# One matmul of each pair in the up projection reads and writes its 512 columns in runs of 64, 16 or 4

## The chip, the cores and the metric

The kernel runs on one core of one Trainium2 chip. The metric is device time in microseconds (us) of one execution, and the number compared is the median over several runs. The profile is of one execution of the same program, taken by the hardware profiler.

## What is computed

One layer of a transformer trunk on 256 tokens of width 2048, in float32: two groups of attention heads on one common projection, then an MLP, then a norm. The part that the change touches is the first product of the MLP, `m @ w_up`:

```python
m = rms_norm(h, mlp_norm)                 # (256, 2048)
h = h + jnp.square(relu(m @ w_up)) @ w_down   # w_up: 2048 x 8192, w_down: 8192 x 2048
return rms_norm(h, final_norm)
```

The MLP's two weight matrices hold 2 x 67 MB and make up most of the 184 MB that the kernel reads.

## The kernel before, in words

**Two halves for each number.** Every product is made in TensorE's fp32r type. So that little precision is lost, each float32 number is split into a hi part (the number rounded to fp32r) and a lo part (the rest, again fp32r). Activations lie transposed, with 128 rows of the model dimension on the partitions, and side by side in the free dimension stand the 256 hi values of the 256 tokens and then their 256 lo values: 512 columns for each block of 128 rows (`split_scaled`, L131, and `split`, L136). Weights come from HBM in parts of 128 x 1024 (`load_part`, L96): a DMA brings the float32 part, ScalarE writes its hi (L101), VectorE its lo (L102).

**One chunk is a pair of matmuls** (`mm_chunk`, L108). With 128 x 128 weights, the first matmul of the pair (L111) takes the hi weights and streams all 512 columns, hi and lo halves of the activations, into the 512 float32 columns of a PSUM bank. The second (L113) takes the lo weights and streams only the 256 hi columns, and it adds to the second half of the bank. A tile (`mm_tile`, L116) is 16 such pairs for the 16 blocks of 2048 rows, all accumulated in one bank. After it `evac_sum` (L126) copies the second half out with ScalarE and VectorE adds the first half.

**The MLP** (L687 to L733) goes through the hidden dimension in four quarters of 2048 (`qd` = 0 to 3). For each quarter, 16 up tiles of 16 pairs are made (tile names `up0_0` to `up3_15`), relu and square are applied, the result is split again into the tiles `us` (tags B and C), and then 16 down tiles (`dn`) of 16 pairs are made and added to the residual `h`. In all, the up projection has 4 x 16 x 16 = 1024 pairs, 256 in a quarter.

**What sets the order.** The instructions are written in program order, and the tile framework adds the semaphores. Weights pass through pools of four buffers each (raw, hi, lo), and four PSUM banks hold dense tiles, so loading and splitting run ahead of TensorE until a buffer is missing.

**The end of the kernel.** The last two down tiles are made apart (L735 to L793). Line 748 makes their lo products: the moving operand is 256 columns lying side by side. Line 741 (`hi_pass`) makes their hi products for one block of 128 tokens: its moving operand is 256 columns too, but in two runs of 128 columns, one from the hi half and one from the lo half, 256 columns apart; its output in PSUM is 256 columns side by side.

In the attention part, line 430 multiplies in plain float32 (not fp32r): two calls of 256 columns for each pair of heads.

Of the kernel before, what the change touches and what calls it, by code (L numbers as in the profile page):

```python
# [16 lines left out]
P = 128  # L17
S = 256
D = 2048
KC = D // P  # L20
# [10 lines left out]
WH = 1024  # L31
# [16 lines left out]
def kernel(  # L48
# [18 lines left out]
    nc = tc.nc  # L67
# [9 lines left out]
    def dense_ps(name):  # L77
        return psd.tile([P, 512], F32, tag="d", name=name)
# [17 lines left out]
    def load_part(src, n, name):  # L96
        raw = wpool.tile([P, WH], F32, tag="raw", name=f"raw_{name}")
        hi = wpool.tile([P, WH], F32R, tag="whi", name=f"hi_{name}")
        lo = wpool.tile([P, WH], F32R, tag="wlo", name=f"lo_{name}")
        nc.sync.dma_start(raw[:, :n], src)  # L100
        nc.scalar.copy(hi[:, :n], raw[:, :n])  # L101
        nc.vector.tensor_tensor(lo[:, :n], raw[:, :n], hi.bitcast(F32)[:, :n], op=ALU.subtract)  # L102
        return hi, lo

    def load_block(src, name):
        return [load_part(src[:, i * WH:(i + 1) * WH], WH, f"{name}_{i}") for i in range(2)]

    def mm_chunk(ps, w, col, act, k, first, last):  # L108
        hi, lo = w[col // WH]
        col = col % WH  # L110
        nc.tensor.matmul(ps[:, 0:2 * S], lhsT=hi[:, col:col + P], rhs=act(k, 0, 2 * S),  # L111
                         start=first, stop=False)
        nc.tensor.matmul(ps[:, S:2 * S], lhsT=lo[:, col:col + P], rhs=act(k, 0, S),  # L113
                         start=False, stop=last)

    def mm_tile(name, w, off, act, ks):  # L116
        ps = dense_ps(name)
        n = len(ks)
        for i, k in enumerate(ks):
            mm_chunk(ps, w, off + i * P, act, k, i == 0, i == n - 1)  # L120
        return ps

    def view(t):
        return lambda k, a, b: t[:, k, a:b]

    def evac_sum(ps, name):  # L126
        t = work.tile([P, S], F32, tag="evt", name=f"t_{name}", bufs=3)
        nc.scalar.copy(t, ps[:, S:2 * S])
        return t
# [6 lines left out]
    def split(dst, src):  # L136
        nc.scalar.copy(dst[:, 0:S], src)
        nc.vector.tensor_tensor(dst[:, S:2 * S], src, dst.bitcast(F32)[:, 0:S], op=ALU.subtract)

    def tmp1(name):  # L140
        return work.tile([P, S], F32, tag="t1", name=name, bufs=5)
# [31 lines left out]
    def square_sum(acc, src, first, name, eng=nc.gpsimd):  # L173
        if first:
            nc.scalar.activation(acc, src, AF.Square)
        else:
            sq = work.tile([P, S], F32, tag="sq", name=f"sq_{name}", bufs=2)
            nc.scalar.activation(sq, src, AF.Square)
            eng.tensor_tensor(acc, acc, sq, op=ALU.add)
# [25 lines left out]
    def bcast_ps(v, name):  # L205
        ps = misc_ps(f"bc_{name}")
        for b in range(2):
            dg = work.tile([P, P], F32, tag="diag", name=f"dg_{name}_{b}", bufs=2)
            nc.vector.tensor_scalar(dg, ident, v[:, b:b + 1], None, op0=ALU.mult)
            nc.tensor.matmul(ps[:, b * P:(b + 1) * P], lhsT=ones, rhs=dg, start=True, stop=True)  # L210
        return ps

    def mean_eps(acc_row, n, name):
        ps = token_sums(acc_row, name)
        v = small(f"ms_{name}")
        nc.vector.tensor_scalar(v, ps[:, 0:2], 1.0 / n, EPS, op0=ALU.mult, op1=ALU.add)
        return v
# [38 lines left out]
    for gi, (c0, n) in enumerate(GROUPS):  # L256
        if gi < 2:
            w = [load_part(w_in0[:, c0 * 512:(c0 + n) * 512], n * 512, f"in0_{c0}")]
        nc.sync.dma_start(h[:, c0:c0 + n, :], xT[:, c0:c0 + n, :])
        if gi == 0:  # L260
            nc.sync.dma_start(g_sb, params)
        if gi >= 2:
            w = [load_part(w_in0[:, c0 * 512:(c0 + n) * 512], n * 512, f"in0_{c0}")]
        for c in range(c0, c0 + n):
            split_scaled(xs[:, c, :], h[:, c, :], g_sb[:, G_ATTN + c:G_ATTN + c + 1])
        for c in range(c0, c0 + n):
            for j in range(4):
                mm_chunk(ps0[j], w, (c - c0) * 512 + j * P, xsv, c, c == 0, c == KC - 1)
        if 1 <= gi <= 5:
            buckets(gi - 1)  # L270
        if gi in (2, 4, 6, 8):
            x_squares(gi // 2 - 1)
# [232 lines left out]
    for i in range(15):  # L505
# [8 lines left out]
        w = load_block(w_in[i], f"in{i}")  # L514
        ps = mm_tile(f"in{i}", w, 0, xsv, list(range(KC)))
# [32 lines left out]
    for b in range(2):  # L548
        w = load_block(w_kn[b], f"kn{b}")
        for j in range(4):  # L550
            ps = mm_tile(f"kn{b}_{j}", w, j * 512, kvv, list(range(LC)))
# [3 lines left out]
    for b in range(2):  # L555
        w = load_block(w_v[b], f"v{b}")
        for tb in range(2):
            ps = dense_ps(f"v{b}_{tb}")
            for k in range(LC):
                hi, lo = w[k // 2]  # L560
# [82 lines left out]
    for n, (b, j) in enumerate((b, j) for b in range(3) for j in range(4)):  # L643
        if j == 0:
            w = load_block(w_q_b[b], f"qb{b}")
        ps = mm_tile(f"qb{b}_{j}", w, j * 512, cqv, list(range(LC)))
# [6 lines left out]
        while todo and n >= todo[0][0]:  # L653
            _, jj, rp = todo.pop(0)
# [4 lines left out]
    def residual(ps, mt):  # L659
        nc.vector.tensor_tensor(h[:, mt, :], ps[:, 0:S], h[:, mt, :], op=ALU.add)  # L660
        nc.vector.tensor_tensor(h[:, mt, :], ps[:, S:2 * S], h[:, mt, :], op=ALU.add)
# [3 lines left out]
    for half in range(2):  # L665
        for b in range(8):
            w = load_block(w_out[half, b], f"wo{half}_{b}")
            for j in range(2):
                mt = 2 * b + j
                ps = mm_tile(f"wo{half}_{mt}", w, j * 1024, view(ys[1 - half]), list(range(8)))  # L670
# [11 lines left out]
    msv = view(ms_box[0])  # L682
# [4 lines left out]
    for qd in range(NQ):  # L687
        us = [big.tile([P, 8, 2 * S], F32R, tag=tg, name=f"us{tg}{qd}") for tg in ("B", "C")]

        def usv(k, a, b, us=us):  # L690
            return us[k // 8][:, k % 8, a:b]

        for j in range(QC):
            w = load_block(w_up[qd * QC + j], f"up{qd}_{j}")
            ps = mm_tile(f"up{qd}_{j}", w, 0, msv, list(range(KC)))
            t = evac_sum(ps, f"up{qd}_{j}")
            nc.vector.tensor_tensor(t, ps[:, 0:S], t, op=ALU.add)
            u = tmp1(f"u{qd}_{j}")
            nc.vector.scalar_tensor_tensor(u, t, 0.0, t, op0=ALU.max, op1=ALU.mult)
            split(us[j // 8][:, j % 8, :], u)  # L700
            if qd == 0 and j == 2:
                v = mean_eps(accm, D, "m")
                nc.vector.tensor_copy(dsm, v)
                dps = bcast_ps(v, "m")
                dm = tmp1("dm")
                nc.vector.tensor_copy(dm, dps[:, 0:S])
            if qd == 0 and 4 <= j < 8:
                k = 4 * (j - 4)
                nc.gpsimd.tensor_tensor(h[:, k:k + 4, :], h[:, k:k + 4, :],
                                        dm.unsqueeze(1).broadcast_to([P, 4, S]), op=ALU.mult)  # L710
        tail = KC - 2 if qd == NQ - 1 else KC
        head = [(load_block(w_down[qd, mt], f"dn{qd}_{mt}"), dense_ps(f"dn{qd}_{mt}"))
                for mt in range(2)]
        for mt, ks in ((0, range(15)), (1, range(4)), (0, range(15, QC)), (1, range(4, QC))):
            w, ps = head[mt]
            for k in ks:
                mm_chunk(ps, w, k * P, usv, k, k == 0, k == QC - 1)
        for mt in range(tail):
            if mt < 2:
                ps = head[mt][1]  # L720
            else:
                w = load_block(w_down[qd, mt], f"dn{qd}_{mt}")
                ps = mm_tile(f"dn{qd}_{mt}", w, 0, usv, list(range(QC)))
            residual(ps, mt)
            if qd == NQ - 1:
                if fin is None:
                    fin = big.tile([P, 2, 2, KC, P], F32, tag="A", name="fin")
                square_sum(acch, h[:, mt, :], mt == 0, f"f{mt}", nc.vector)
                if mt == 1:
                    nc.scalar.activation(warm, acch[:, 0:1], AF.Sqrt)  # L730
                nc.scalar.activation(fin[:, 0, :, mt, :],
                                     h[:, mt, :].rearrange("p (b c) -> p b c", b=2), AF.Copy,
                                     scale=g_sb[:, G_FIN + mt:G_FIN + mt + 1])  # L733
# [11 lines left out]
    for mt, w, ps in last:  # L745
        o = misc_ps(f"dn_lo{mt}")[:, 0:S]
        for k in range(QC):
            nc.tensor.matmul(o, lhsT=w[k // 8][1][:, (k % 8) * P:(k % 8 + 1) * P],
                             rhs=us[k // 8][:, k % 8, 0:S], start=(k == 0), stop=(k == QC - 1))
# [145 lines left out]
```

## Time and profile before

| | |
|---|---|
| median of 3 runs | 1037.45 us |
| all runs | 1034.93, 1037.45, 1048.86 us |
| span of the profiled execution, first to last instruction | 1034.7 us |
| TensorE matmul busy | 1007.2 us, 97% of the span |
| VectorE busy | 713.2 us, 69% |
| ScalarE busy | 540.3 us, 52% |
| GpSimd busy | 109.6 us, 11% |
| read from HBM | 183.7 MB |

The profiled execution's own time is known by its span, 1034.7 us. The lowest run is 0.2 us above it and the median 2.8 us. In the trace, a matmul's duration covers its way through the array and overlaps the next one: a 512-column matmul is shown with 391 ns, but the next begins after 230 ns. What a stream of matmuls takes is therefore read from start to start, in the timeline or in the chain of waits.

### The profile page before, as it was taken

How to read it: one execution, taken by the hardware profiler on the slowest of the kernel's cores; microseconds unless marked ns; L12 is line 12 of the kernel's file. 1: busy time of each engine (PE TensorE's matmuls, PEld its weight loads, DVE VectorE, ACT ScalarE, POOL GpSimd, SP SyncE). 2: the span in 40 equal slices, each digit the busy share in tenths (PEclk: the TensorE clock that was granted, in tenths of full speed). 3: DMA queues.
4: the chain of work that ended last, by engine and by line, in shares of the span. 5: the costliest groups of instructions: out<-in, count | busy, mean ns of one | idle time of the engine just before them, and what ended most of it. 6: DMA issues, size and time to landing. Idle time of an engine off the chain costs nothing.

```text
span 1034.7 us, 15469 instructions
## 1 busy us (share of the span) xinstructions
PE 1007.2 (97%) x5830; PEld 881.8 (85%) x5830; DVE 713.2 (69%) x1123; ACT 540.3 (52%) x893; POOL 109.6 (11%) x117
## 2 busy tenths in 40 slices
PE   6889899999999999999999999999999999999997
PEld 5768788889888888888888888888888888888887
DVE  7985888698897866556666656566666556666664
ACT  7464898875664444333444433344443334445553
POOL 4222321452132200000000000000000000000000
PEclk9999999999999999999999999999999999999999
DMA  7579434564455655655656555556655656666652
GB/s 261 171 227 245 133 113 128 168 195 142 153 189 167 204 185 186 198 185 193 191 186 192 194 183 191 193 186 190 194 186 190 195 185 189 196 185 190 194 167 82
DMA packets 53163, 188.94 MB, mean 183 GB/s; under 512 B 6065, under 2 KB 6449, under 8 KB 52833
## 3 DMA queue, kind: packets, MB, share of 16 engines
q1 hardware_dynamic: 51696, 182.54, 55.2%
q0 software_dynamic: 1392, 5.41, 2.2%
q8 instruction: 46, 0.75, 0.3%
q14 instruction: 29, 0.23, 0.1%
HBM read 183.70 MB, written 4.23 MB: 182 GB/s over the span
## 4 chain that ended last, share of the span: by engine, by line
PE 88%; DMA 4%; DVE 3%; ACT 2%; issue 1%; SPq 0%; POOL 0%; POOLq 0%; ACTq 0%; DVEq 0%
PE up L111 23%; PE dn L111 22%; PE up L113 12%; PE dn L113 11%; PE wo L111 6%; PE wo L113 3%; PE in L111 2%; DMA raw_in<-in_w_in_dram 2%; DMA bias<-bias_scratch 2%; PE in L113 1%; DVE lo_in L102 1%; PE dn L741 1%; PE yp L430 1%; PE kn L111 1%; DVE buck L235 1%
## 5 line engine op out<-in xcount | busy, mean ns | idle before, releaser
L111 PE MATMUL up<-ms,hi_up 128*128 128x512 f32 x1024 | 355.8, 392 | 0.0
L113 PE MATMUL up<-ms,lo_up 128*128 128x256 f32 x1024 | 286.8, 280 | 0.0
L102 DVE TENSOR_TENSOR lo_up<-raw_up,hi_up 128x1024 fp32r<-128x1024 f32 x128 | 161.2, 1260 | 115.0 <-ACT hi_up L101 114.5
L101 ACT CAST hi_dn<-raw_dn 128x1024 fp32r<-128x1024 f32 x128 | 135.0, 1054 | 200.8 <-PE dn L111 160.7
L101 ACT CAST hi_up<-raw_up 128x1024 fp32r<-128x1024 f32 x128 | 134.6, 1052 | 178.0 <-issue 133.8
L111 PEld LDWEIGHTS up<-ms,hi_up 128*128 128x128 f32 x1024 | 191.5, 187 | 42.2
L102 DVE TENSOR_TENSOR lo_dn<-raw_dn,hi_dn 128x1024 fp32r<-128x1024 f32 x128 | 156.9, 1226 | 96.3 <-ACT hi_dn L101 91.0
L113 PEld LDWEIGHTS up<-ms,lo_up 128*128 128x128 f32 x1024 | 193.5, 189 | 0.0
L111 PE MATMUL dn<-usB,hi_dn 128*128 128x512 f32 x496 | 174.9, 391 | 0.0
L111 PE MATMUL dn<-usC,hi_dn 128*128 128x512 f32 x496 | 174.9, 391 | 0.0
L113 PE MATMUL dn<-usB,lo_dn 128*128 128x256 f32 x496 | 138.9, 280 | 0.0
L113 PE MATMUL dn<-usC,lo_dn 128*128 128x256 f32 x496 | 138.9, 280 | 0.0
L111 PE MATMUL in<-xs,hi_in 128*128 128x512 f32 x304 | 111.4, 406 | 9.4 <-DVE xs L133 8.6
L111 PEld LDWEIGHTS dn<-usB,hi_dn 128*128 128x128 f32 x496 | 92.8, 187 | 20.3
L111 PEld LDWEIGHTS dn<-usC,hi_dn 128*128 128x128 f32 x496 | 92.8, 187 | 20.3
L113 PEld LDWEIGHTS dn<-usB,lo_dn 128*128 128x128 f32 x496 | 93.7, 189 | 0.0
L113 PEld LDWEIGHTS dn<-usC,lo_dn 128*128 128x128 f32 x496 | 93.7, 189 | 0.0
L111 PE MATMUL wo<-ys,hi_wo 128*128 128x512 f32 x256 | 91.1, 398 | 0.0
L113 PE MATMUL in<-xs,lo_in 128*128 128x256 f32 x304 | 86.8, 287 | 3.1 <-DVE lo_in L102 3.1
L111 PEld LDWEIGHTS in<-xs,hi_in 128*128 128x128 f32 x304 | 58.5, 193 | 23.3 <-DVE xs L133 8.0
L113 PE MATMUL wo<-ys,lo_wo 128*128 128x256 f32 x256 | 72.2, 283 | 0.0
L113 PEld LDWEIGHTS in<-xs,lo_in 128*128 128x128 f32 x304 | 58.8, 194 | 5.4 <-DVE lo_in L102 4.6
(295 smaller groups left out, 1217.9 us busy)
## 6 DMA issues: line engine op xcount, KB each, us to landing
raw_up<-in_w_up_dram SPq DMA_DIRECT2D x128, 512.0 KB, 4.4
raw_dn<-in_w_down_dram SPq DMA_DIRECT2D x128, 512.0 KB, 4.4
raw_in<-in_w_in_dram SPq DMA_DIRECT2D x37, 512.0 KB, 5.5
raw_wo<-in_w_out_dram SPq DMA_DIRECT2D x32, 512.0 KB, 3.8
raw_qb<-in_w_q_b_dram SPq DMA_DIRECT2D x6, 512.0 KB, 4.3
bias_scratch<-biasT POOLq DMA_DIRECT2D x4, 512.0 KB, 5.1
bias<-bias_scratch POOLq DMA_DIRECT2D x4, 512.0 KB, 9.8
raw_kn<-in_w_kn_dram SPq DMA_DIRECT2D x4, 512.0 KB, 4.1
```

What stands on the lines that cost most here:

```text
L101: nc.scalar.copy(hi[:, :n], raw[:, :n])
L102: nc.vector.tensor_tensor(lo[:, :n], raw[:, :n], hi.bitcast(F32)[:, :n], op=ALU.subtract)
L111: nc.tensor.matmul(ps[:, 0:2 * S], lhsT=hi[:, col:col + P], rhs=act(k, 0, 2 * S), start=first, stop=False)
L113: nc.tensor.matmul(ps[:, S:2 * S], lhsT=lo[:, col:col + P], rhs=act(k, 0, S), start=False, stop=last)
L235: nc.vector.scalar_tensor_tensor(buck, n_f[:, 0:2, :], float(thr), buck, op0=ALU.is_ge, op1=ALU.add)
L430: nc.tensor.matmul(yp[:, 0:S], lhsT=v_sc[:, 0, t // 4, j, :], rhs=pt[:, j, 0:2, :].rearrange("p i c -> p (i c)"), start=(j == 0), stop=False)
L741: nc.tensor.matmul(ps[:, b * S:(b + 1) * S].rearrange("p (a c) -> p a c", a=2), lhsT=hi[:, (k % 8) * P:(k % 8 + 1) * P], rhs=x[:, :, b, :] ...
```

## The change

For the quarters `qd` = 1, 2 and 3 the up tiles are made by a new function, `mm_runs`, in place of `mm_tile`. It issues the same pairs in the same order with the same weights. Only the first matmul of a pair differs: its 512 moving columns, and in the same way its 512 output columns in PSUM, are taken in another order. In place of 0 to 511 it takes a run of columns from the hi half, the run at the same place of the lo half, the next run of the hi half, and so on. A run has 64 columns in quarter 1, 16 in quarter 2 and 4 in quarter 3 (256, 64 and 16 bytes). Since input and output are permuted alike, each result lands at the same place of PSUM as before. Quarter 0, the second matmul of each pair, and all else stay as they are.

In the built program, 768 rows of TensorE's list have another shape: 256 each of 128x4x2x64, 128x16x2x16 and 128x64x2x4 in place of 128x512. No row is added, removed or moved on any engine, and no row waits for anything else.

```diff
+    def mm_runs(name, w, act, ks, run):
+        ps = dense_ps(name)
+        n = len(ks)
+
+        def runs(t):
+            return t.rearrange("p (a b c) -> p b a c", a=2, c=run)
+
+        for i, k in enumerate(ks):
+            hi, lo = w[i * P // WH]
+            col = i * P % WH
+            nc.tensor.matmul(runs(ps[:, 0:2 * S]), lhsT=hi[:, col:col + P],
+                             rhs=runs(act(k, 0, 2 * S)), start=(i == 0), stop=False)
+            nc.tensor.matmul(ps[:, S:2 * S], lhsT=lo[:, col:col + P], rhs=act(k, 0, S),
+                             start=False, stop=(i == n - 1))
+        return ps
...
             w = load_block(w_up[qd * QC + j], f"up{qd}_{j}")
-            ps = mm_tile(f"up{qd}_{j}", w, 0, msv, list(range(KC)))
+            if qd == 0:
+                ps = mm_tile(f"up{qd}_{j}", w, 0, msv, list(range(KC)))
+            else:
+                ps = mm_runs(f"up{qd}_{j}", w, msv, list(range(KC)), (64, 16, 4)[qd - 1])
             t = evac_sum(ps, f"up{qd}_{j}")
```

## Rows read from the trace of the kernel before

**Rows 1.** The page: busy time by engine, and the granted clock in 40 slices.

```profile
PE 1007.2 (97%) x5830; PEld 881.8 (85%) x5830; DVE 713.2 (69%) x1123; ACT 540.3 (52%) x893; POOL 109.6 (11%) x117
...
PEclk9999999999999999999999999999999999999999
```

**Rows 2.** The page: the chain that ended last, by engine and by line.

```profile
PE 88%; DMA 4%; DVE 3%; ACT 2%; issue 1%; SPq 0%; POOL 0%; POOLq 0%; ACTq 0%; DVEq 0%
PE up L111 23%; PE dn L111 22%; PE up L113 12%; PE dn L113 11%; PE wo L111 6%; PE wo L113 3%; PE in L111 2%; DMA raw_in<-in_w_in_dram 2%; DMA bias<-bias_scratch 2%; PE in L113 1%; DVE lo_in L102 1%; PE dn L741 1%; PE yp L430 1%; PE kn L111 1%; DVE buck L235 1%
```

**Rows 3.** Busy time by engine in four stretches, the up projection's quarters.

```profile
core 0: us, PE busy (x) PEld busy (x) DVE busy (x) ACT busy (x) POOL busy (x), PEclk, DMA share, GB/s
311.00:401.10 90.10, 90.10 (x523) 79.19 (x522) 66.55 (x88) 43.06 (x64) 12.90 (x6) 1.00 0.58 187
489.80:578.60 88.80, 88.80 (x515) 78.30 (x514) 56.51 (x79) 42.25 (x62) 0.00 (x0) 1.00 0.60 190
667.30:756.10 88.80, 88.80 (x515) 78.31 (x514) 56.51 (x79) 42.24 (x62) 0.00 (x0) 1.00 0.60 190
844.80:933.50 88.70, 88.70 (x514) 78.20 (x513) 56.47 (x79) 42.24 (x62) 0.00 (x0) 1.00 0.60 190
```

**Rows 4.** Who waited for whom, all engines: total us, times, longest.

```profile
ACT hi_dn L101 <- PE dn L111: 160.7, 94, 2.8
...
ACT hi_up L101 <- PE up L111: 20.3, 13, 1.8
```

**Rows 5.** Timeline of PE, quarter 1's first pairs and its end: start, duration, instruction.

```profile
489.81 0.39 PE L111 MATMUL up<-ms,hi_up 128*128 128x512 f32 x1
490.04 0.28 PE L113 MATMUL up<-ms,lo_up 128*128 128x256 f32 x1
490.16 0.39 PE L111 MATMUL up<-ms,hi_up 128*128 128x512 f32 x1
490.39 0.28 PE L113 MATMUL up<-ms,lo_up 128*128 128x256 f32 x1
...
578.56 0.39 PE L111 MATMUL dn<-usB,hi_dn 128*128 128x512 f32 x1
```

**Rows 6.** The chain near the end: start us, us, what.

```profile
1011.36 3.83 PE dn_lo L748 x32
1015.19 3.84 PE dn L741 x32
```

**Rows 7.** The chain in the attention part, plain float32.

```profile
131.10 0.86 PE yp L430 x4
```

**Rows 8.** Timeline of PE, second pair of the kernel.

```profile
7.11 0.63 PE L111 MATMUL in<-xs,hi_in 128*128 128x512 f32 x1
7.54 0.41 PE L113 MATMUL in<-xs,lo_in 128*128 128x256 f32 x1
```

## The prediction

> **What bounds the kernel now.** I read the page first: TensorE is busy 97% of the span, and the clock row shows the same digit in all 40 slices [rows 1]. The chain that ended last comes next: 88% of it is TensorE's own work, and the largest line is the very one that the change edits, the up projection's first matmul, L111, with 23% of the span [rows 2]. Then the stage itself: in each of the four quarters of the up projection TensorE is busy for the whole stretch, at a granted clock of 1.00, the upper of its two levels, while VectorE works 56 of 89 us, ScalarE 42, and the DMA engines are at 0.60 [rows 3]. So nothing feeds TensorE late there. The list of waits says it from the other side: ScalarE's split of the next weights stands still for 160.7 us in all until a down matmul lets a buffer go, and for 20.3 us until an up matmul does [rows 4]. The other engines wait for TensorE. Hence a rule for the sum: what an up matmul gets longer is added to the end in full, with no cover, and what it gets shorter is taken off in full while the slack of the others lasts.
>
> **What one matmul costs.** Durations in the timeline overlap, so I go by starts. In quarter 1 the first matmul of a pair begins at 489.81 and the second at 490.04, 0.23 us later. The quarter's 256 pairs run from 489.81 to 578.56, 88.75 us, or 0.347 us a pair [rows 5]; that leaves 0.117 us for the second matmul. The edited matmuls are 3 x 256 = 768, and 768 x 0.23 = 177 us of the kernel runs in them. One column takes 0.23 us / 512 = 0.45 ns.
>
> **The change, part by part.**
>
> *Instructions.* None is added, removed or moved, on any queue, and no wait changes. Weights, PSUM banks and the columns that VectorE and ScalarE read afterwards stay the same. All of this costs 0, and it needs no cover, because no work is added.
>
> *The order of the columns.* This is the only term: how long does a matmul take whose 512 columns come, and go, in 8 runs of 64, 32 runs of 16 or 128 runs of 4, in place of one run? The trace of before has no such matmul. The nearest row is the kernel's end. L748 streams 256 columns lying side by side, and 32 of these take 3.83 us; L741 streams 256 columns in two runs, hi half and lo half, and 32 of these take 3.84 us [rows 6]. One break in the reading therefore costs 0.01 / 32 = 0.3 ns by these rows, which is their rounding: nothing that can be seen. Two limits of this row have to be said. L741 breaks its reading only, its output lies side by side, and no matmul of the trace has breaks in what it writes. And both lines start a matmul every 0.12 us, a little over the 0.117 us of the pair's second matmul, so something beside the column stream may set their pace and hide a small break.
>
> *Bounds.* Above: the slowest 512-column matmul near by is at the kernel's start, 7.11 to 7.54, 0.43 us, half the pace [rows 8]. At that pace an edited matmul is 0.20 us longer: 256 x 0.20 = 51 us if only runs of 4 fall to it, 768 x 0.20 = 154 us if all three do. In between lies a stall of one column for each break: 7 + 31 + 127 = 165 breaks over the three lengths, x 256 matmuls x 0.45 ns = 19 us. Below: the plain-float32 matmuls of L430 leave four records in 0.86 us, 0.215 us each [rows 7]; this is the quickest pace of a full pass that I find, and if another order of columns brought the fp32r matmuls to it, the gain would be 0.015 x 768 = 11.5 us. I take 0, because the row with the same operands, type and pair of halves (L741) shows 0, and because the three lengths differ from it only in how many breaks there are. The ends, -11.5 and +154 us, are kept for the range.
>
> [...] No row here shows a broken write to PSUM. [...]
>
> **The sum.** Span 1034.7 + 0 = 1034.7 us. The median of the runs stood 2.8 us above this span (1037.45 to 1034.7), so I forecast 1037.5 us for the median.
>
> **The rivals.**
>
> 1. *A stall of about one column at each break.* For: 512 columns take 0.230 us while a plain-float32 pass takes 0.215, so an fp32r stream already seems to run at what its operand supply gives, and there is no reserve for an interruption. Against: [rows 6] show 0.3 ns for a break, within their rounding. Price 19 us, of which 127 / 165, or 15 us, falls in quarter 3: 1056.5 us, +1.8%. At two columns a break it would be 1075 us.
>
> 2. *Runs of 4 are too short, longer ones not* (the one that ends slower). The mechanism: operands are fetched, or sums put down, in pieces longer than 16 bytes, so that in quarter 3 half of every piece is thrown away and the matmul falls to half pace. Its place is the stretch that now runs from 844.8 to 933.5 us, which would grow by 51 us to 140 us; quarters 1 and 2 would stay at 88.8. The time is 1037.5 + 51 = 1088.5 us. It decides the sign from about 0.08 us per matmul on (2% is 20.7 us; over 256 matmuls 0.081 us each, a third more than now). For: the missing reserve named under 1, and that no row has a run shorter than 128. Against: nothing in the trace names such a piece. [...]
>
> 3. *Any break in the order halves the pace*, at the write into PSUM, where each matmul adds to sums that now lie out of order. All 768 matmuls take 0.43 us: 1037.5 + 154 = 1191.5 us, each of the three quarters 140 us. For: broken writes occur nowhere in this trace. Against: [rows 6] show that a broken read alone does not do it. [...]
>
> 4. *The mixed order is quicker*, with up to 11.5 us gained: 1026 us, -1.1%. For: the 0.015 us between the two paces. Against: nothing says that the order is what costs them. Even in full it is within 2%.
>
> 5. *The order asked for is not what the engine does*, for instance because the runs are joined again. The built instructions carry the broken shapes, which speaks against it; the time would be that of no change.
>
> **How the numbers follow.** No cost: 0.57, at 1037.5 us, its own range 1034 to 1045 from the spread of the runs shown. Rival 1: 0.11, rival 2: 0.16, rival 3: 0.09, rival 4: 0.04, rival 5: 0.03. A measurement of this kernel tells about 2%, 20.7 us, from no change. Faster by more than that asks for more than rival 4 can give: 0.01. Slower takes rivals 2 and 3 and the part of rival 1 above one column a break, 0.16 + 0.09 + 0.03 = 0.28. The rest is within 2%: 0.71. The range runs from 1031 to 1090 us: below, it leaves out half of rival 4 (0.02); above, rival 3 (0.09) and the part of rival 2 that is worse than half pace (0.05); in all 0.16.
>
> **What the changed profile would show.** Right: in all three quarters the first matmul's start to the second's is 0.23 us as in quarter 0, each quarter lasts 88.7 to 88.8 us, and TensorE still has no wait there. Rival 1: the distance grows with the number of breaks, about 0.233, 0.244 and 0.287 us for 64, 16 and 4. Rival 2: 0.23, 0.23 and about 0.43. Rival 3: 0.43 in all three. Rival 4: under 0.23. The second matmul of a pair is not edited and should stay at 0.117; if it grows, the cost is not in the order of its own columns but in what the first leaves behind. I would be wrong in the premise, not only in the size, if the quarters get longer while the distances stay, because then something waits that has slack now.

## The result, and the profile after

The changed kernel took 1049.74 us in the median of 20 runs (1044.3 to 1054.87), the kernel before 1046.72 us in 20 runs (1031.11 to 1049.67). The ratio is 1.0119, with a 95% interval of 1.0087 to 1.0151, where no change was forecast. To read it one has to know that the runs of the kernel before fall into two groups, here 8 runs at 1031.11 to 1037.45 us and 12 at 1046.05 to 1049.67 us, and that the ratio counts the lower group and only those two runs of the upper one that lie within 1.5% of the fastest run. Taken over all runs the medians are 0.3% apart; against the lower group alone (median 1033.9 us) the changed kernel is 15.9 us or 1.5% slower. None of its runs lies in that group. The profile of before that stands above is of the lower group.

In the profile after, the chain of waits looks the same. TensorE makes up 88% of it again, and by line, answering to [rows 2], the edited matmul (L126 now) has taken over most of the place of the up projection's L111:

```profile
PE dn L111 22%; PE up L126 18%; PE dn L113 11%; PE up L128 9%; PE up L111 6%; PE wo L111 5%; PE up L113 3%; PE wo L113 3%; PE in L111 2%; DMA bias<-bias_scratch 2%; DMA raw_in<-in_w_in_dram 1%; PE in L113 1%; DVE lo_in L102 1%; PE dn L760 1%; DVE buck L251 1%
```

Between 330 and 1020 us TensorE still waits for nothing, as before. So the time went into the matmuls themselves. The four quarters of the up projection, which answer to [rows 3] and have the same columns:

```profile
308.50:399.60 91.10, 91.10 (x523) 79.12 (x522) 67.07 (x89) 43.14 (x64) 13.43 (x6) 1.00 0.53 185
490.05:580.50 90.45, 90.45 (x514) 78.45 (x513) 56.49 (x79) 42.22 (x62) 0.00 (x0) 1.00 0.52 186
670.95:763.10 92.15, 92.15 (x514) 79.10 (x513) 56.47 (x79) 42.17 (x62) 0.00 (x0) 1.00 0.52 183
853.55:945.75 92.20, 92.20 (x514) 78.61 (x513) 56.52 (x79) 43.20 (x62) 0.00 (x0) 1.00 0.52 183
```

The granted clock is 1.00 in all of them. Quarter 1 (runs of 64) grew from 88.8 to 90.45 us, quarters 2 and 3 (runs of 16 and of 4) from 88.8 to 92.2. Thirty-one breaks in a matmul cost the same as 127. That is no price for each break.

The second surprise is outside the edit. To see it, one counts matmuls in stretches of equal length, each inside one stage. A pair is two matmuls, so in 80 us the pace is 160 divided by the count: 463 or 464 mean 0.345 us, 455 mean 0.352, 446 mean 0.359 (a little low, because matmuls that straddle an edge count too; from the starts of the stages the three paces are 0.3467, 0.3533 and 0.360 us a pair). These rows have the stretch, its length, PE's busy time with the count in brackets, the granted clock, and the DMA's share and rate. In the profile after, they are the down stage of quarter 0, the up and down stages of quarter 1, and so on to the last down stage:

```profile
402.00:482.00 80.00, 80.00 (x455) 1.00 0.52 185
495.00:575.00 80.00, 80.00 (x455) 1.00 0.52 184
585.00:665.00 80.00, 80.00 (x455) 1.00 0.53 187
675.00:755.00 80.00, 80.00 (x446) 1.00 0.51 182
767.00:847.00 80.00, 80.00 (x455) 1.00 0.54 188
860.00:940.00 80.00, 80.00 (x447) 1.00 0.52 184
946.00:1024.00 78.00, 78.00 (x443) 1.00 0.52 176
```

The down stages were not edited, and here they go at 0.353 us a pair, like quarter 1. In the profile of before, the same code went at 0.347:

```profile
402.00:482.00 80.00, 80.00 (x463) 1.00 0.60 191
495.00:575.00 80.00, 80.00 (x464) 1.00 0.60 189
```

So the stream of pairs has a quicker and a slower steady pace with the same instructions, at the same granted clock, and the trace of before holds both. Its quarter 0 began like this:

```profile
310.99 0.40 PE L111 MATMUL up<-ms,hi_up 128*128 128x512 f32 x1
311.23 0.28 PE L113 MATMUL up<-ms,lo_up 128*128 128x256 f32 x1
311.35 0.40 PE L111 MATMUL up<-ms,hi_up 128*128 128x512 f32 x1
...
312.05 0.40 PE L111 MATMUL up<-ms,hi_up 128*128 128x512 f32 x1
```

Three pairs from 310.99 to 312.05 are 1.06 us, 0.353 a pair; after the small float32 matmuls near 329 us that same profile went over to 0.347. The profile after went into the same place at 0.347 and came out of it at 0.353. This much of the difference between the two profiles began before the first edited matmul, so it can't be charged to the change from these two traces alone.

### The profile page after: what moved, and what is told of

The parts are those of the page before. It is cut to its first block, busy times and chain, and to the rows that moved or that the text cites. A ratio compares the mean times of both kernels' runs of the same rounds, so it can differ in the third digit from the quotient of the medians.

```text
span 1047.8 us, 15469 instructions
## 1 busy us (share of the span) xinstructions
PE 1022.5 (98%) x5830; PEld 883.5 (84%) x5830; DVE 712.9 (68%) x1123; ACT 540.3 (52%) x893; POOL 110.1 (11%) x117
## 4 chain that ended last, share of the span: by engine, by line
PE 88%; DMA 4%; DVE 3%; ACT 3%; issue 1%; SPq 0%; POOL 0%; DVEq 0%; POOLq 0%; ACTq 0%
PE dn L111 22%; PE up L126 18%; PE dn L113 11%; PE up L128 9%; PE up L111 6%; PE wo L111 5%; PE up L113 3%; PE wo L113 3%; PE in L111 2%; DMA bias<-bias_scratch 2%; DMA raw_in<-in_w_in_dram 1%; PE in L113 1%; DVE lo_in L102 1%; PE dn L760 1%; DVE buck L251 1%
## 5 line engine op out<-in xcount | busy, mean ns | idle before, releaser
L126 PE MATMUL up<-ms,hi_up 128*128 128x512 f32 x768 | 274.9, 402 | 0.0
L128 PE MATMUL up<-ms,lo_up 128*128 128x256 f32 x768 | 216.8, 282 | 0.0
L111 PE MATMUL dn<-usC,hi_dn 128*128 128x512 f32 x496 | 178.2, 399 | 0.0
L111 PE MATMUL dn<-usB,hi_dn 128*128 128x512 f32 x496 | 178.2, 399 | 0.0
L126 PEld LDWEIGHTS up<-ms,hi_up 128*128 128x128 f32 x768 | 145.4, 189 | 38.6
L128 PEld LDWEIGHTS up<-ms,lo_up 128*128 128x128 f32 x768 | 144.6, 188 | 0.0
L111 PE MATMUL in<-xs,hi_in 128*128 128x512 f32 x304 | 111.4, 406 | 9.7 <-DVE xs L149 9.1
L111 PEld LDWEIGHTS dn<-usC,hi_dn 128*128 128x128 f32 x496 | 93.2, 188 | 23.2
L111 PEld LDWEIGHTS dn<-usB,hi_dn 128*128 128x128 f32 x496 | 93.2, 188 | 23.2
L111 PE MATMUL up<-ms,hi_up 128*128 128x512 f32 x256 | 90.4, 398 | 0.0
L111 PE MATMUL wo<-ys,hi_wo 128*128 128x512 f32 x256 | 90.4, 396 | 0.0
L111 PEld LDWEIGHTS in<-xs,hi_in 128*128 128x128 f32 x304 | 58.5, 193 | 23.9 <-DVE xs L149 8.0
```

The costliest lines, as they stand in the source:

```text
L126: nc.tensor.matmul(runs(ps[:, 0:2 * S]), lhsT=hi[:, col:col + P], rhs=runs(act(k, 0, 2 * S)), start=(i == 0), stop=False)
```

## The experiments

All kernels are the changed kernel with the edit shown (lines left out are marked by dots), and stand beside runs of the kernel before on the same chip. The kernels of e_rw, e_len and e_near ran once each, at 1046.98, 1073.85 and 1046.0 us; they are read by their profiles alone.

### e_rw: reading or writing?

```diff
-    def mm_runs(name, w, act, ks, run):
+    def mm_runs(name, w, act, ks, run, rd, wr):
...
-            nc.tensor.matmul(runs(ps[:, 0:2 * S]), lhsT=hi[:, col:col + P],
-                             rhs=runs(act(k, 0, 2 * S)), start=(i == 0), stop=False)
+            o, x = ps[:, 0:2 * S], act(k, 0, 2 * S)
+            nc.tensor.matmul(runs(o) if wr else o, lhsT=hi[:, col:col + P],
+                             rhs=runs(x) if rd else x, start=(i == 0), stop=False)
...
-                ps = mm_runs(f"up{qd}_{j}", w, msv, list(range(KC)), (64, 16, 4)[qd - 1])
+                ps = mm_runs(f"up{qd}_{j}", w, msv, list(range(KC)), 4, qd != 2, qd != 1)
```

> Runs of 4 everywhere, but in quarter 1 only the moving operand is read in runs and the output lies side by side, in quarter 2 only the output is written in runs, in quarter 3 both. Quarters 1 and 2 put sums in the wrong order, so the output is not the reference's. Theory R (the read order sets the pace): quarter 1 goes at 0.360 us a pair (92.2 us), quarter 2 at the pace of its unedited neighbours, 0.347 or 0.353 us (88.8 or 90.5 us), quarter 3 at 0.360. Rival W (the write order sets it): quarter 1 at 0.347 or 0.353, quarters 2 and 3 at 0.360. Rival C (0.360 is one more pace that a stage falls into by chance): no tie to the side that is broken; an unedited stage may show 0.360 too.

Measured: down stage 0, quarter 1 (reads in runs), down stage 1, quarter 2 (writes in runs), down stage 2, quarter 3 (both):

```profile
400.00:480.00 80.00, 80.00 (x463) 1.00 0.56 190
490.00:570.00 80.00, 80.00 (x446) 1.00 0.52 183
585.00:665.00 80.00, 80.00 (x455) 1.00 0.54 188
675.00:755.00 80.00, 80.00 (x455) 1.00 0.54 187
765.00:845.00 80.00, 80.00 (x455) 1.00 0.54 185
855.00:935.00 80.00, 80.00 (x446) 1.00 0.52 182
```

Reading alone gives 0.360; writing alone keeps the pace of its neighbours, 0.353. Theory R holds and W falls. Rival C falls too: no unedited stage in the profiles of this document goes at 0.360. The stream entered quarter 1 at 0.347 and the unedited stage behind it went at 0.353: a first sign that the edited quarter sets the pace of what follows. Whether broken writes would end the quicker pace stays open here, since quarter 2 was entered at the slower one.

### e_write: broken writes, entered at the quicker pace

As e_rw, but only the output is in runs of 4 in quarters 1 and 2, and both sides in quarter 3:

```diff
-                ps = mm_runs(f"up{qd}_{j}", w, msv, list(range(KC)), 4, qd != 2, qd != 1)
+                ps = mm_runs(f"up{qd}_{j}", w, msv, list(range(KC)), 4, qd == 3, True)
```

> Runs of 4 in the output alone in quarters 1 and 2 (the moving operand is read side by side; these sums land in the wrong order, so the output is not the reference's), in input and output in quarter 3. Theory (the write order has no part in it): where the stream enters quarter 1 at 0.347 us a pair, it stays there through quarter 1, the down stage, quarter 2 and the next down stage; only quarter 3 goes at 0.360 and the last down stage at 0.353: about 1031 to 1037 + 3.4 + 1.5 = 1036 to 1042 us. Rival (broken writes cost nothing by themselves at the slower pace but end the quicker one): 0.353 from quarter 1 on, about 1044.

Measured, in the same order of stages up to quarter 3:

```profile
400.00:480.00 80.00, 80.00 (x463) 1.00 0.58 191
490.00:570.00 80.00, 80.00 (x464) 1.00 0.59 190
580.00:660.00 80.00, 80.00 (x464) 1.00 0.58 190
670.00:750.00 80.00, 80.00 (x463) 1.00 0.59 188
...
850.00:930.00 80.00, 80.00 (x446) 1.00 0.57 182
```

Writes in 128 runs of 4 neither cost anything nor end the quicker pace: both quarters stay at 0.347, the down stages beside them too, and only quarter 3, where the reads are broken too, falls to 0.360. The profiled span is 1037.8 us. The ten timed runs lie at 1037.96 to 1039.84 and at 1047.32 to 1053.23, the kernel before beside them at 1030.95 to 1035.56, 1040.67, and 1044.32 to 1050.79.

### e_len: runs of 32, 8 and 2

```diff
-                ps = mm_runs(f"up{qd}_{j}", w, msv, list(range(KC)), (64, 16, 4)[qd - 1])
+                ps = mm_runs(f"up{qd}_{j}", w, msv, list(range(KC)), (32, 8, 2)[qd - 1])
```

> Runs of 32, 8 and 2 in quarters 1, 2 and 3, read and written. Theory S (a step, not a price for each break): 8 and 2 go at 0.360 us a pair like 16 and 4 (92.2 us), and 32 goes either with 64 (0.347 or 0.353) or with 16 (0.360), which places the step. Rival P (a price for each break): from 32 to 2 the breaks grow from 15 to 255, so the pair gets longer from quarter to quarter; with runs of 2 it would be above 0.36 by more than it is with runs of 4. Rival L (pieces of 16 bytes): 8 as 16, but 2 (8 bytes) at about half pace, 0.43 us for the edited matmul, over 120 us for the quarter.

Measured, quarters 1, 2 and 3, and a pair in the third from the timeline of PE:

```profile
490.00:570.00 80.00, 80.00 (x446) 1.00 0.53 183
...
675.00:755.00 80.00, 80.00 (x446) 1.00 0.54 184
...
855.00:935.00 80.00, 80.00 (x345) 1.00 0.42 144
```

```profile
899.83 0.51 PE L126 MATMUL up<-ms,hi_up 128*128 128x512 f32 x1
900.17 0.29 PE L128 MATMUL up<-ms,lo_up 128*128 128x256 f32 x1
900.29 0.51 PE L126 MATMUL up<-ms,hi_up 128*128 128x512 f32 x1
```

Runs of 32 and of 8 go at 0.360 like 16 and 4, so from 15 to 127 breaks it is one step, and the step lies between runs of 64 and of 32. Rival P falls for these. Runs of 2 are another matter: 0.34 us from the first matmul to the second, +0.11, and the quarter took 119.4 us (851.37 to 970.76). Rival L was right that runs of 8 bytes are too short, with half of its price. Input and output are both broken here: that reading is the cause was shown for runs of 4 (e_rw, e_write) and is assumed for the other lengths.

### e_r64: runs of 64 alone

```diff
-                ps = mm_runs(f"up{qd}_{j}", w, msv, list(range(KC)), (64, 16, 4)[qd - 1])
+                ps = mm_runs(f"up{qd}_{j}", w, msv, list(range(KC)), 64)
```

> Runs of 64 in all three quarters. Theory (64 costs nothing, and the unedited stream has two paces, 0.347 and 0.353 us a pair, that are settled before the edit by chance): times fall in the same two groups as those of the kernel before, about 1031 to 1037 and 1046 to 1050 us, ratio 1.00. Rival (any break ends the quicker pace): the quicker group is missing and all runs lie at 1040 us or above, ratio about 1.01.

Measured: 1036.53 us in the median of 12 (1031.69 to 1052.9), before 1035.09 (1032.24 to 1037.61); ratio 1.0018 (0.9993 to 1.0043). All three quarters counted 463 or 464 in 80 us, 0.347 a pair, and so did the down stages; the span was 1030.7 us. Quarters 1, 2 and 3:

```profile
490.00:570.00 80.00, 80.00 (x463) 1.00 0.55 190
...
670.00:750.00 80.00, 80.00 (x464) 1.00 0.56 191
...
845.00:925.00 80.00, 80.00 (x464) 1.00 0.56 191
```

Runs of 64 cost nothing, and seven breaks left the quicker pace alone in this profile. Two of the 12 runs, 1047.04 and 1052.9 us, lie in the upper group, where none of the 17 runs of before beside them does; so few runs can't tell this from chance.

### e_r16q1: runs of 16 in quarter 1 alone

```diff
-            if qd == 0:
+            if qd != 1:
                 ps = mm_tile(f"up{qd}_{j}", w, 0, msv, list(range(KC)))
             else:
-                ps = mm_runs(f"up{qd}_{j}", w, msv, list(range(KC)), (64, 16, 4)[qd - 1])
+                ps = mm_runs(f"up{qd}_{j}", w, msv, list(range(KC)), 16)
```

> Runs of 16 in quarter 1 alone; quarters 0, 2 and 3 as before. Theory K (a stage at 0.360 also throws the stream out of the quicker pace for the rest): runs that begin quickly take 1031 to 1037 + 3.4 for the quarter + 8.5 for five later stages at 0.353 in place of 0.347, about 1043 to 1049; runs that begin slowly 1047 + 1.7, about 1049; nothing under 1040. Rival N (the cost stays in the quarter): the quick group is there, at 1034 to 1040 us.

Measured: 1048.47 us (1047.68 to 1051.76, 5 runs) against 1035.09; ratio 1.014 (1.0121 to 1.0159). Down stage 0, quarter 1, and the next four stages, none of them edited:

```profile
408.00:488.00 80.00, 80.00 (x463) 1.00 0.54 190
500.00:580.00 80.00, 80.00 (x446) 1.00 0.52 183
590.00:670.00 80.00, 80.00 (x455) 1.00 0.53 186
...
860.00:940.00 80.00, 80.00 (x455) 1.00 0.54 188
```

Theory K holds: the quarter itself costs 3.4 us (92.16 for 88.75), and all unedited stages behind it pay 1.7 us each (90.45 for 88.75; the last, shorter one 1.5). By its stages one edited quarter costs 11.7 us here, more than the three of the change together (10 us in the next run, entered at the quicker pace too): it comes a quarter earlier, so more unedited stages lie behind it.

### e_again: the changed kernel once more

No edit.

> The changed kernel once more, beside runs of the kernel before on the same chip. Theory K (quarter 2 at 0.360 us a pair ends the quicker pace of the unedited stages behind it): where a run enters quarter 1 at 0.347, quarters 0 and 1 and the down stages between them stay there, quarter 2 takes 92.2 us, and from there the unedited stages go at 0.353: 1031 to 1037 + 3.4 + 1.7 + 3.4 + 1.5 = 1041 to 1047 us; where it enters at 0.353, about 1050. Rival N (each edited quarter pays 3.4 us and the unedited stages none): 1031 to 1037 + 6.8, about 1038 to 1044, with 0.347 in the down stages behind quarters 2 and 3.

Measured: 1044.23 us (1044.01 to 1046.52, 6 runs) against 1036.22 (1032.64 to 1045.71, 23 runs); ratio 1.0084 (1.0062 to 1.0106). This time the stream entered the edited part at the quicker pace:

```profile
490.00:570.00 80.00, 80.00 (x464) 1.00 0.53 189
580.00:660.00 80.00, 80.00 (x463) 1.00 0.55 191
670.00:750.00 80.00, 80.00 (x446) 1.00 0.53 182
760.00:840.00 80.00, 80.00 (x455) 1.00 0.53 184
855.00:935.00 80.00, 80.00 (x446) 1.00 0.52 183
```

Quarter 1 and the down stage behind it keep 0.347. From the trace's starts, quarter 2 takes 92.16 us (+3.4), the down stage behind it 90.44 (+1.7), quarter 3 92.20 (+3.45) and the last long down stage 79.13 for 77.65 (+1.5): 10 us in sum, a third of it in stages that the edit doesn't touch. The span was 7.6 us above that of the profile of before (1042.3 to 1034.7), the rest being 1.9 us less ahead of the MLP and 0.5 us less at the end. Rival N falls.

Where a run enters the edited part at the slower pace, as the profile after did, only the step from 0.353 to 0.360 is left to pay, 1.7 us in each of quarters 2 and 3. The 20 runs of the first comparison look like a mixture of both cases, 6 at 1044.3 to 1046.54 us and 14 at 1048.1 to 1054.87 us; only one of them was profiled, at 1049.55 us.

### e_one16: a single matmul with runs of 16

```diff
+            f = runs if i == 0 else (lambda t: t)
-            nc.tensor.matmul(runs(ps[:, 0:2 * S]), lhsT=hi[:, col:col + P],
-                             rhs=runs(act(k, 0, 2 * S)), start=(i == 0), stop=False)
+            nc.tensor.matmul(f(ps[:, 0:2 * S]), lhsT=hi[:, col:col + P],
+                             rhs=f(act(k, 0, 2 * S)), start=(i == 0), stop=False)
...
-            if qd == 0:
+            if qd == 0 or j > 0:
                 ps = mm_tile(f"up{qd}_{j}", w, 0, msv, list(range(KC)))
             else:
-                ps = mm_runs(f"up{qd}_{j}", w, msv, list(range(KC)), (64, 16, 4)[qd - 1])
+                ps = mm_runs(f"up{qd}_{j}", w, msv, list(range(KC)), 16)
```

> Only 3 matmuls are changed: the very first of quarters 1, 2 and 3 has runs of 16; all else is as in the kernel before. Theory K1 (two paces are both stable, and one disturbed matmul is enough to end the quicker one): the stages from quarter 1 on go at 0.353 us a pair in place of 0.347, 5.9 stages x 1.7 us = 10 us, about 1042 to 1047 us, though not one matmul there is longer. Rival K2 (it takes a whole stretch of edited pairs): the profile shows 0.347 throughout, time as before, ratio within 0.3% of 1.

Measured: 1040.53 us in the median of 12 runs (1032.19 to 1051.92), before 1036.11 in 23 (1031.02 to 1051.94). Six runs lie at 1032 to 1037.3, which K1 forbids; the other six lie at 1043.76 to 1051.92, as do 7 of the 23 runs of before. The profile was already at 0.353 in down stage 0, ahead of the first edited matmul, so it shows nothing on K1. One such matmul does not regularly end the quicker pace; how many it takes was not tried. The profile shows two other things. Three single matmuls with runs of 16 do not bring the quicker pace back: from 333 us on, every stage stays at 0.353. And it is the only profile of this code at the slower pace throughout, all but three matmuls as before: its stages from quarter 0 on last 12.8 us longer than those of the profile of before, of 13.9 us between the two spans. So the pace accounts for nearly all of the distance between these two profiles, one of either group; no run of the kernel before itself was profiled in the upper one.

### e_one2: a single matmul with runs of 2

The same edit with 2 in place of 16:

```diff
-                ps = mm_runs(f"up{qd}_{j}", w, msv, list(range(KC)), 16)
+                ps = mm_runs(f"up{qd}_{j}", w, msv, list(range(KC)), 2)
```

> As the kernel with one matmul of runs of 16 at the head of each of quarters 1 to 3, but with runs of 2: each of the 3 is some 0.11 us longer by itself, 0.33 us in all. After a whole quarter of runs of 2 the stream came out at the quicker pace, after 16 and 4 at the slower. Theory (the way out of the disturbance settles the pace, and runs of 2 lead to the quick one): 0.347 after each of the three, time as before, ratio 1.00. Rival (any disturbance ends the quicker pace): 0.353 after the first, ratio about 1.01. Third (it is chance each time): both paces among the three.

Measured: 1037.77 us (1032.55 to 1043.46, 12 runs), before 1036.11 in 23. The profile has 0.347 before and after each of the three; the quarters last 88.87 us, 0.12 more than 88.75, which is the price of the one matmul. So a matmul that is half as long again does not end the quicker pace. None of the 12 runs lies above 1043.5, while 7 of the 23 runs of before beside it lie at 1044.77 to 1051.94, as do 6 of the 12 with single matmuls of runs of 16 at the same places, from 1043.76 us on. That asked for the next test.

### e_back: can one matmul bring the quicker pace back?

The edit of e_one2, but with runs of 16 in the whole of quarter 1, and single matmuls with runs of 2 at the head of quarters 2 and 3.

```diff
...
-            if qd == 0:
+            if qd == 0 or (qd > 1 and j > 0):
                 ps = mm_tile(f"up{qd}_{j}", w, 0, msv, list(range(KC)))
             else:
-                ps = mm_runs(f"up{qd}_{j}", w, msv, list(range(KC)), (64, 16, 4)[qd - 1])
+                ps = mm_runs(f"up{qd}_{j}", w, msv, list(range(KC)), *((16,) if qd == 1 else (2, 1)))
```

The last argument is the length of the runs and, where a second number follows, how many matmuls of the tile get the broken order.

> Runs of 16 in all of quarter 1, as in the kernel that had them there alone (1048 us), and a single matmul with runs of 2 at the head of quarter 2 and of quarter 3. Theory (the paces are steady states, and one matmul with runs of 2, itself 0.11 us longer, brings the stream back to the quicker one): the down stage behind quarter 1 at 0.353, quarter 2 and all behind it at 0.347; about 1031 to 1037 + 3.4 + 1.7 + 0.2 = 1037 to 1042 us. Rival (one matmul settles nothing, or runs of 2 keep a quick stream quick but don't make a slow one quick): 0.353 to the end, about 1048 us.

Measured: 1041.78 us (1037.92 to 1045.09, 12 runs; ratio 1.0052, 1.0031 to 1.0072), where the kernel with quarter 1 alone took 1048.47 (ratio 1.014). Six of the runs lie above the 1042 us that the theory gave. Quarter 1, the down stage behind it, quarter 2 and the next down stage:

```profile
495.00:575.00 80.00, 80.00 (x446) 1.00 0.53 183
590.00:670.00 80.00, 80.00 (x454) 1.00 0.54 188
680.00:760.00 80.00, 80.00 (x464) 1.00 0.55 191
765.00:845.00 80.00, 80.00 (x463) 1.00 0.54 191
```

The theory holds in the profile: a stage at 0.353, one matmul of 0.32 us, and 0.347 to the end. The paces are two steady ones of the same instructions, 0.353 and 0.347 us a pair, and a single matmul moved the stream from the slower to the quicker. Whether the order of its columns does this or the 0.1 us that it is longer was not tested apart.

### e_near: another broken order

```diff
...
-            return t.rearrange("p (a b c) -> p b a c", a=2, c=run)
+            return t.rearrange("p (a b c) -> p b a c", b=jump // run, c=run)
...
-                ps = mm_runs(f"up{qd}_{j}", w, msv, list(range(KC)), (64, 16, 4)[qd - 1])
+                ps = mm_runs(f"up{qd}_{j}", w, msv, list(range(KC)), *((16, 32), (16, 64), (32, 64))[qd - 1])
```

> Another broken order of the same 512 columns, read and written, that does not alternate between hi and lo half: runs of 16 whose next run lies 32 columns on (quarter 1), runs of 16 with the next 64 on (quarter 2), runs of 32 with the next 64 on (quarter 3). Theory B (what counts is how often the read breaks off): all three at 0.360 us a pair, 92.2 us a quarter. Rival D (what counts is the distance of 256 columns between the two halves): they go at 0.347 or 0.353, 88.8 or 90.5 us.

Measured: quarter 1 took 92.16 us, 0.360 a pair, with jumps of 32 columns; quarter 2 took 89.61, or 0.350, and quarter 3 took 90.45, or 0.353, both with jumps of 64. Quarters 1, 2 and 3:

```profile
495.00:575.00 80.00, 80.00 (x446) 1.00 0.52 183
...
675.00:755.00 80.00, 80.00 (x459) 1.00 0.55 188
...
855.00:935.00 80.00, 80.00 (x454) 1.00 0.53 185
```

Quarter 2 keeps its pace from its first pairs to its last, so 0.350 is no mean of 0.347 and 0.353. Quarter 3 shows no cost that could be told from the pace at which it was entered: the unedited stage ahead of it went at 0.353 too. But the down stage behind it, from 942.91 us on, went at 0.347, so runs of 2 are not the only way back to the quicker pace. The alternation between hi and lo half is therefore not needed for the slow step, but length and number of the runs don't decide alone either: runs of 16 go at 0.360 or at 0.350 by where the next run lies. Neither theory holds as it was put.

### e_cure and e_cure2: four such matmuls in the kernel before

```diff
...
-            if qd == 0:
+            if j != (4 if qd == 0 else 0):
                 ps = mm_tile(f"up{qd}_{j}", w, 0, msv, list(range(KC)))
             else:
-                ps = mm_runs(f"up{qd}_{j}", w, msv, list(range(KC)), (64, 16, 4)[qd - 1])
+                ps = mm_runs(f"up{qd}_{j}", w, msv, list(range(KC)), 2, 1)
```

The last two arguments are the length of the runs and the number of matmuls of the tile that get the broken order.

> The kernel before with 4 matmuls of runs of 2: one in quarter 0's fifth tile, behind the small float32 matmuls of that quarter, and one at the head of each of quarters 1, 2 and 3; 0.4 us for the four. Theory (each brings the stream to the quicker pace): no run above about 1041 us, while some runs of the kernel before lie at 1044 to 1052; median at or below that of before. Rival (chance): the same share of runs at 1044 and above as the kernel before.

> The kernel before with 4 single matmuls of runs of 2 once more, to see it beside runs of the kernel before that fall into both groups of times, if this chip shows them. Theory (each of the four brings the stream to the quicker pace): no run above about 1041 us, the median below that of before by as much as before has runs at 1044 to 1052. Rival (it does nothing): the same share of such runs in both.

Measured first: 1036.38 us (1033.6 to 1040.25, 12 runs) against 1036.22; only 1 of 23 runs of before lay above 1044, so there was nothing to cure, and this tells only that the four matmuls cost too little to be seen (ratio 0.9995, 0.9974 to 1.0015). The second time 13 of the 23 runs of before lay at 1044.32 to 1050.79, and none of the 12 of this kernel (1032.42 to 1042.21). That none of the 12 falls there by chance, at the share of before, is unlikely (less than 1 in 1000). The medians are 1034.91 and 1045.24 us, 10.3 us or 1.0% apart; the median of the ten other runs of before is 1033.71 us, so the gain is in the upper group alone. The trace shows the one in quarter 0 at work:

```profile
330.02 0.40 PE L111 MATMUL up<-ms,hi_up 128*128 128x512 f32 x1
...
332.14 0.40 PE L111 MATMUL up<-ms,hi_up 128*128 128x512 f32 x1
...
332.49 0.49 PE L127 MATMUL up<-ms,hi_up 128*128 128x512 f32 x1
332.81 0.29 PE L129 MATMUL up<-ms,lo_up 128*128 128x256 f32 x1
...
333.29 0.39 PE L127 MATMUL up<-ms,hi_up 128*128 128x512 f32 x1
...
334.68 0.39 PE L127 MATMUL up<-ms,hi_up 128*128 128x512 f32 x1
```

Six pairs from 330.02 to 332.14 are 2.12 us, 0.353 a pair. The matmul at 332.49 is the one with runs of 2. Four pairs from 333.29 to 334.68 are 1.39 us, 0.347 a pair. No edit but the order of one matmul's columns lies between the two. The other three single matmuls of this profile met the stream at 0.347 and left it there. This kernel loses nothing that can be seen against the kernel before, and its median is 1.0% lower where 13 of 23 runs of that kernel lie in the upper group; these are two chips, and no others were tried.

## Why the prediction was wrong

- **What bounds the kernel** was right. TensorE streams without a wait, and what a matmul gets longer comes out at the end in full: 10 us more in the stages of e_again, less what other stretches differ.
- **"I take 0, because the row with the same operands, type and pair of halves (L741) shows 0"** is the step that failed. [Rows 6] compared one break with none, at 0.12 us per matmul. The prediction said itself that something beside the column stream may set that pace; it should then not have served as the value. The reason that followed, that the three lengths differ from that row "only in how many breaks there are", failed as well. Seven breaks do cost 0 (e_r64, 0.347 us a pair), fifteen to 127 cost one step when hi and lo half alternate, 0.360 us a pair for 0.347, 3.4 us a quarter; and 31 breaks cost that step or 0.350 by where the next run lies (e_near).
- **The pace of the unedited matmuls was taken as one number**, 0.347 us [rows 5]. The trace of before held a second, 0.353, at 311 us, which was not read. So a second term was put at nothing: a part of the cost (1.7 + 1.5 of 10 us in e_again, 8.3 of 11.7 us in e_r16q1 by its stages) lies in stages whose instructions did not change, and no sum over edited instructions can find it.
- **The base** was one of two. The forecast of 1037.5 us is the span plus what the median of three runs stood above it; one of those three, 1048.86 us, lay in the upper group, and the forecast's own range of 1034 to 1045 us left it out. Over 20 runs the median of before is 1046.72 us. Of the 12.2 us between 1037.5 and 1049.74 us, 9.3 separate that base from this median. What is left to the change hangs on the pace at which a run enters it: 10 us from 0.347, some 3.4 us from 0.353. That 1049.74 us lies between 1031 and 1090 us is luck: the room above 1045 us was kept for rivals 1 and 2, which did not come.
- **Rival 1**, one column of stall a break, gave 19 us, twice what the change cost by its stages, with the wrong law: quarters 2 and 3 would have differed by the factor of four in breaks, and they are equal.
- **Rival 2** had the right kind of limit, but at runs of 2 and not of 4: +0.11 us for each of those matmuls, half again; whether at the read or at the write was not tested for this length. They took 0.34 us in place of 0.23 (e_len), while the quarters with runs of 32 to 4 shared one pace, 0.360 us a pair. Pieces in which operands are fetched or sums put down, the mechanism that the rival gave, are shown by no run.
- **Rival 3**, broken writes, is excluded: two quarters of e_write wrote in 128 runs at 0.347 us a pair, as with output side by side.
- **Rivals 4 and 5** found no support: no order was quicker than 0.347, and the broken order is carried out, as the steps show.
- **The sign that the prediction set for itself** told only half: it said that a growing second matmul would mean that the cost is not in the order of the first one's columns but in what it leaves behind. At 0.360 a pair in the profile after, the second grew from 0.117 to 0.121 us, but the first from 0.230 to 0.239, so two thirds of the step lie in the edited matmul itself.

Open: what makes the paces. They are 0.3467, 0.350, 0.3533 and 0.360 us a pair, within rounding whole multiples of 3.33 ns; no run shows why. Why the step lies between runs of 64 and 32, why for runs of 16 a jump of 64 columns is milder than one of 32 or 256 (e_near), and why a quarter at 0.360 was left at 0.353 all 12 times in these profiles, stays open too. So does what the small float32 matmuls of quarter 0 do to the pace: across them it went from 0.353 to 0.347 us a pair in the profile before, and from 0.347 to 0.353 in the one after.

## What to carry to other kernels

Before an instruction's price is taken from a trace, read the same instruction's spacing in all stages, not in one: two values for the same code, as 0.347 and 0.353 us a pair here, mean that the pace has a state, and a change can move that state for the stages behind it, as it did in e_again and e_r16q1. When a kernel's times fall into two groups, count instructions per stretch in both and look for the first stage that differs. Taking the columns of operand and output in runs of 64 was free here (0.347 us a pair, e_r64) and runs of 32 to 4, alternating between the halves, were not (0.360, e_len and e_again), while the order of the writes into PSUM alone, in runs of 4, did not matter (0.347, e_write).

## What the runs showed of the hardware

- A stream of pairs of fp32r matmuls (512 and 256 columns, 128 x 128 weights) ran at 0.3467 or at 0.3533 us a pair with the same instructions, at a granted clock of 1.00 both times, and kept either for hundreds of microseconds (0.3467 from 400 to 1010 us in the profile before, 0.353 from 333 us on in that of e_one16).
- Runs of 32, 16, 8 and 4 float32 columns, alternating between two halves 256 columns apart, gave 0.360 us a pair, runs of 64 no loss (0.347); runs of 2 gave 0.466 (119.4 us for 256 pairs). Input and output were in runs alike; for runs of 4 the input alone was enough. Runs of 16 with the next run 64 columns on gave 0.350.
- A single matmul with runs of 2 took 0.32 us in place of 0.23 (e_back and e_cure2; 0.34 in a whole quarter of them, e_len), and moved the stream from 0.353 to 0.347 both times a profile caught it at the slower pace (e_back and e_cure2); entered at 0.347, it left it there. Three with runs of 16 left the stream at 0.353 (e_one16).
- Output written in 128 runs of 4 columns, alternating between the halves of a PSUM bank, took the same time as output side by side: 464 and 463 matmuls in 80 us, 0.347 us a pair (e_write).
